# A hybrid attention and recurrence layer: the K/V block leaves PSUM bank by bank, and the second half of the recurrence gets its gates later

## The chip, the cores and the metric

The kernel runs on one core of one Trainium2 chip. The metric is the device time of one execution in microseconds (us), lower is better. The core has five engines with an instruction queue each: TensorE (PE in the profile; its weight loads are listed as PEld), VectorE (DVE), ScalarE (ACT), GpSimd (POOL) and SyncE (SP), which here only issues the DMA transfers of weights, x and the output. SBUF is the working memory. PSUM, where TensorE writes its products, has eight banks of 512 float32 values a partition.

## The reference

One layer of an encoder on 512 tokens of width 2048: a norm, one wide input projection, attention and a gated linear recurrence side by side, and one output projection.

```python
h = rms_norm(x, norm_w)
proj = jnp.einsum('bsd,de->bse', h, w_in)
q, k, v, g_attn, xr, g_lru = jnp.split(proj, SPLITS, axis=-1)
attn_out = attention_group(q, k, v, q_norm_w, k_norm_w)
lru_out = lru_group(xr, conv_w, conv_b, lru_wa, lru_ba, lru_wx, lru_bx, lru_lambda)
mixed = jnp.concatenate([rms_norm(attn_out, attn_norm_w) * jax.nn.silu(g_attn),
                         rms_norm(lru_out, lru_norm_w) * jax.nn.silu(g_lru)], axis=-1)
return x + jnp.einsum('bse,ed->bsd', mixed, w_out)
```

Attention has 8 query heads and 2 key/value heads of 128 features; q and k are normed head by head and rotated. The recurrence has 1024 features in 8 blocks of 128: a convolution over four tokens gives xc, then for each of two directions

```python
r = jax.nn.sigmoid(block_diag(xf, wa) + ba)
i = jax.nn.sigmoid(block_diag(xf, wx) + bx)
log_a = -LRU_C * r * jax.nn.softplus(-lam)
a = jnp.exp(log_a)
mult = jnp.sqrt(-jnp.expm1(2.0 * log_a))
return linear_scan(a, mult * (i * xf), reverse)
```

and the two directions are added. All of it is float32.

## The kernel before, in words

**Products.** Each float32 operand is split into a high and a low part, and `mm3` (L111 to L114) adds up three products, high by high, high by low and low by high. Weights come in as chunks of 256 rows by 512 columns (`wraw`, L155); ScalarE writes each half's high part (`wh`, L168) and VectorE subtracts it to get the low part (`wl`, L169). `wh` and `wl` have four slots, so two chunks are in hand at a time: a chunk can be split once the chunk two before it has been multiplied.

**Projections.** `proj_tok` (L271, by `tok_block`, L259) makes a block of 512 output columns for all tokens: four PSUM banks, the tag `pj`, one bank for each tile of 128 tokens. It runs over eight chunks, and in each chunk over the four token tiles; it yields after each tile, which is one *step* of six products. So a projection has 32 steps, and its four banks are finished in the last four steps, one after the other. There are only four `pj` banks: the next projection's first step needs the first bank empty, its second step the second bank, and so on. The block from column `C_K` holds the keys (256 columns) and the values (256 columns).

**The order.** TensorE runs its instructions as they are written (`manual_schedule`, L602). `weave(fill, chain)` (L274) interleaves: the chain yields how many steps of the projection go before its next piece. On ScalarE, VectorE and GpSimd a planner orders the instructions when the program is built: among those that it takes to be ready, the one with the best rank goes next. The rank is the place in the program, unless `tc.high_priority` gives a better one: without a number the very best, with `AHEAD` 600 instructions earlier. The queues then run in that order, each in turn; an instruction that is not ready holds those behind it.

**Around the change.** While the K/V block is projected (`a3`), the second half of the recurrence runs woven in (`lru_half(1, a2)`, L650): blocks 4 and 5 as one pair, 6 and 7 as the next (`lru_pair`, L338). A pair first gets its convolution (ScalarE L349, VectorE L354) and its operands split (`gh`, `gl` L344 and L345; `ch`, `cl` L359 and L360). Then each of its two blocks yields its number of steps and has twelve products for the gates into the `mm` banks, which ScalarE empties by four sigmoids (L371); VectorE multiplies `i` by xc (L375). Then ScalarE does four tanh (L380), four exponentials (L386) and two square roots (L390), each kind with a table load, and VectorE the rest of the pair: L393, L394, four scans (L397) and two additions (L401). ScalarE squares the result (L405) and GpSimd adds it up (L406). The steps are

```python
yield from lru_pair(4 * half + b, xrs[bs], grs[bs], (6 + 2 * half, 4, 8, 4)[bs])
```

so in the second half 8, 4, 8 and 4 steps go before the gates of its four blocks, and eight steps come behind the last gates.

**The K/V block leaves PSUM.** `kv(a3)` (L478) starts when the projection is done. It has the best rank, and takes two operations on ScalarE and one on VectorE from each bank: the keys scaled by the token's 1/rms (L432, 256 columns), the high part of the values (L485, 256 columns) and their low part (L486, VectorE, from the same bank). Then `norm_rope` (L438) norms and rotates the keys: squares on ScalarE (L446), 1/rms on GpSimd (L220, L221) and the rotation on VectorE (L451, L453, L459, L460). It is ranked behind the scans of the recurrence, which stand earlier in the program. `kv` is woven into the next projection, Q (`a4`): twenty steps, then the keys of head 0 are transposed on TensorE (L471, one product for each token tile), two more steps, then those of head 1.

Of the kernel before, what the change touches and what calls it, by code (L numbers as in the profile page):

```python
# [13 lines left out]
ALU = mybir.AluOpType  # L14
# [37 lines left out]
def hybrid_kernel(  # L52
# [62 lines left out]

# [1 line left out]
    ident = const([P, P], "ident")  # L117
# [25 lines left out]
    def columns(dst, src):  # L143
        """Vectors staged a row each, turned into a column each."""
        n = src.shape[0]
        pt = mm()
        nc.tensor.transpose(pt[:, :n], src, ident[:n, :n])
        with tc.high_priority():
            nc.vector.tensor_copy(dst, pt[:, :n])
# [3 lines left out]

# [1 line left out]
    def wraw(w, r0, c0, nk=1):  # L155
        """w[r0 : r0 + 2 * P, c0 : c0 + 512], in nk transfers."""
        raw = sb.tile([P, 2, SEQ], F32, tag="wr", bufs=3, name=nm("wr"))
        src = w[r0 : r0 + 2 * P, c0 : c0 + SEQ].rearrange("(k p) e -> p k e", p=P)
        for k in range(nk):
            ks = slice(k * 2 // nk, (k + 1) * 2 // nk)  # L160
            nc.sync.dma_start(raw[:, ks, :], src[:, ks, :])
            yield raw

    def wsplit(raw, k):
        """A row block's float32r high and low parts."""
        hi = sb.tile([P, SEQ], F32R, tag="wh", bufs=4, name=nm("wh"))
        lo = sb.tile([P, SEQ], F32R, tag="wl", bufs=4, name=nm("wl"))
        nc.scalar.copy(hi, raw[:, k, :])  # L168
        nc.vector.tensor_sub(lo, raw[:, k, :], f(hi))  # L169
        return hi, lo  # L170
# [5 lines left out]

# [1 line left out]
    xh, xl = [None] * KT, [None] * KT  # L178
    ssq = const([P, NT, KT // 2], "ssq")

    def xload(c, nk=1):
        """Two column blocks of x, in nk transfers."""
        xc = b4(shape=(P, NT, 2 * P))
# [34 lines left out]
    def rsqrt_mean(dst, src, n, width):  # L218
        """dst = (src / n + EPS) ** -0.5, for few elements."""
        nc.gpsimd.tensor_scalar(dst, src, 1.0 / n, EPS, op0=ALU.mult, op1=ALU.add)  # L220
        nc.gpsimd.tensor_tensor(dst, dst, nhalf[:, :width], op=ALU.pow)  # L221
# [14 lines left out]

# [1 line left out]
    # Generators that yield after every six products, to have other work woven in.  # L238
    def proj_feat(c0, acc, first=None):
        """Four [feature, token] blocks from column c0 on."""  # L240
        acc += [pj() for _ in range(4)]
# [17 lines left out]
    def tok_block(acc, w, r0, c0, lh, ll, nk):  # L259
        """Four [token, feature] blocks of 512 columns of w from c0 on."""  # L260
        acc += [pj() for _ in range(NT)]
# [12 lines left out]
    def weave(fill, chain):  # L274
        """chain yields how many steps of fill go before its next piece."""
        for n in chain:
# [6 lines left out]

# [1 line left out]
    c1 = const([P, 2 * NB], "c1")  # L285
    c2 = const([P, 2 * NB], "c2")

    def lru_consts():
        # c1 = -8 softplus(-lambda), c2 = c1 / 2, by log1p(y) = 2 atanh(y / (2 + y))
        lam = vec[:, R_LAM : R_LAM + 2 * NB]  # L290
# [13 lines left out]
        nc.vector.tensor_mul(acc, acc, s)  # L304
        # softplus(-lam) = 2 acc + max(-lam, 0)
        nc.vector.tensor_scalar(a, lam, -1.0, 0.0, op0=ALU.mult, op1=ALU.max)
# [7 lines left out]
    def evac_bc(acc):  # L314
        """Feature-major blocks out of PSUM, scaled by each token's 1 / rms."""
        res = []
# [7 lines left out]
    def lru_half(half, acc):  # L324
        """Four blocks of the recurrence, two at a time."""
        grs = []
# [7 lines left out]
        for b in range(0, 4, 2):  # L334
            bs = slice(b, b + 2)
            yield from lru_pair(4 * half + b, xrs[bs], grs[bs], (6 + 2 * half, 4, 8, 4)[bs])

    def lru_pair(n0, xrs, grs, steps):  # L338
        """Blocks n0 and n0 + 1; yields before each block's gate products."""
        xcs, cs, rs, is_, ths = [], [], [], [], []  # L340
# [21 lines left out]
        for b, n in enumerate((n0, n0 + 1)):  # L362
# [11 lines left out]
            i = is_[b]  # L374
            nc.vector.tensor_mul(i, i, xcs[b][:, None, :].broadcast_to([P, 2, SEQ]))  # L375
        for b, n in enumerate((n0, n0 + 1)):
            ths.append(b4())
# [5 lines left out]
        for b, n in enumerate((n0, n0 + 1)):  # L383
            for d in range(2):
                j, r = d * NB + n, rs[b][:, d, :]
                last = nc.scalar.activation(r, r, AF.Exp, scale=c1[:, j : j + 1])  # L386
        # sqrt(1 - a^2) = (1 + a) sqrt(-tanh(log_a / 2))
        with tc.issue_after(last.ins):
# [18 lines left out]

# [1 line left out]
    rq = const([P, NT, 2, HD], "rq")  # L409
# [15 lines left out]

    def evac_tok(acc, cols):
        """Token-major blocks out of PSUM, scaled by each token's 1 / rms."""
        res = []
        with tc.high_priority():
            for t in range(NT):  # L430
                e = ev()
                nc.scalar.activation(  # L432
                    e[:, :cols], acc[t][:, :cols], AF.Identity, scale=rstd[:, t : t + 1]
                )
                res.append(e)
        return res

    def norm_rope(es, nh, tab):  # L438
        """The heads of every token tile normed and rotated, in place."""
        es = [e[:, : nh * HD].rearrange("p (h d) -> p h d", d=HD) for e in es]  # L440
# [26 lines left out]
    def turn(rot, h):  # L467
        """The four token tiles of head h, transposed and split."""
        pt = mm()
# [7 lines left out]

    def kv(acc):  # L478
        es = evac_tok(acc, NKV * HD)
        with tc.high_priority():  # L480
            for t in range(NT):
                vv = acc[t][:, NKV * HD :]
                vt = const([P, 2, NKV * HD], f"v{t}", F32R)
                vh[t], vl[t] = vt[:, 0, :], vt[:, 1, :]
                nc.scalar.activation(vh[t], vv, AF.Identity, scale=rstd[:, t : t + 1])  # L485
                nc.vector.scalar_tensor_tensor(  # L486
                    vl[t], vv, rstd[:, t : t + 1], f(vh[t]), op0=ALU.mult, op1=ALU.subtract
                )
        rot = norm_rope(es, NKV, rk)
        for h in range(NKV):  # L490
            yield (20, 2)[h]
# [7 lines left out]
    def turned(rot, h):  # L499
        """Head h's queries, transposed and split."""  # L500
        q = b4(F32R)
# [3 lines left out]
    def weights(q, g, t):  # L505
        """Softmax over the keys for token tile t."""
        qh, ql = q
# [21 lines left out]
    def values(h, half, pth, ptl):  # L529
        """Head h's sums over the keys, for half of the tokens."""  # L530
        gs = slice(h // G * HD, (h // G + 1) * HD)
# [15 lines left out]
    def attention(rots):  # L547
        """All heads, as a pipeline over their token tiles."""
        qs, ps_, pts = {h: turned(rots[0], h) for h in range(2)}, {}, {}
# [18 lines left out]

# [1 line left out]
    mh, ml = [None] * 16, [None] * 16  # L570

    def gate(gs, dst, row):
        """dst *= w * silu(g), in place, in steps."""
        ss = []
# [13 lines left out]
    def group_rstd(sums, name, n):  # L588
        """Per-token 1 / rms of a head group from its feature-major sums of squares."""
        pr = mm()  # L590
# [8 lines left out]

# [1 line left out]
    # TensorE runs its instructions in the order in which they stand here.  # L601
    ctx.enter_context(tc.manual_schedule(engines={mybir.EngineType.PE}))  # L602
# [45 lines left out]
    rope_consts()  # L648
    fill = proj_tok(C_K, a3)
    weave(fill, lru_half(1, a2))  # L650
    drain(fill)
    fill = proj_tok(C_Q, a4)
    weave(fill, kv(a3))
    drain(fill)

    rots = [norm_rope(evac_tok(a4, SEQ), G, rq)]
    drain(proj_tok(C_Q + SEQ, a5))
    rots.append(norm_rope(evac_tok(a5, SEQ), G, rq))

# [44 lines left out]
def _rope_table():  # L704
    """[SEQ, 2, HD]: the cosines, and the sines with the sign that goes with the swapped halves."""
    s = np.arange(SEQ)
# [36 lines left out]
```

## Time and profile before

| | |
|---|---|
| three runs | 683.22, 682.63, 683.08 us |
| median | 683.08 us |
| profiled execution, span from first to last instruction | 681.7 us |
| profiled execution, whole time | not listed beside the span; the median is 1.4 us above the span |
| TensorE products | busy 671.0 us (98%) |
| VectorE / ScalarE / GpSimd | busy 409.0 / 318.8 / 79.7 us |
| granted TensorE clock, mean | 0.996 of full speed |

The profile is one execution taken by the hardware profiler. Its page gives the busy time of each engine, the span in 40 slices, the DMA queues, the chain of work that ended last, and the costliest groups of instructions. Beside the page, the trace answers questions: who waited for whom (engine and line waited for: us in total, times, longest), a timeline of one engine (start in us, duration in us, engine, line, operation, result <- operands, shapes, count, and in brackets how long the engine had been idle and what ended that), and the busy time of each engine in a stretch of time. L12 is line 12 of the kernel. Names are the pools' tags: `pj` and `mm` are PSUM banks, `ev`, `b` and `k` are buffers in SBUF, `v` the split values. A product's duration overlaps the next one's, so the pace of TensorE is read from the starts.

### The profile page before, as it was taken

To read this page: it belongs to the slowest core of one execution; us is meant where nothing else is said; L and a number is where in the kernel's file an instruction comes from. 1 tells how busy PE (TensorE), PEld (TensorE's weight loads), DVE (VectorE), ACT (ScalarE), POOL (GpSimd) and SP (SyncE) were. 2 spreads that over 40 slices of the span, in tenths; PEclk is the share of its full clock that TensorE was granted. 3 is DMA by queue.
4 is the path that set the end of the run, shared out by engine and by line. 5 is a ranking of instruction groups with operands and counts; after the bars stand their busy time and mean duration, and the time that the engine had idled before them with its cause. 6 is when DMAs were issued, how large, how long until landed. Compare 5 with 4: busy or idle time off the path is not lost.

```text
span 681.7 us, 8574 instructions
## 1 busy us (share of the span) xinstructions
PE 671.0 (98%) x3149; PEld 557.3 (82%) x3149; DVE 409.0 (60%) x713; ACT 318.8 (47%) x593; POOL 79.7 (12%) x84
## 2 busy tenths in 40 slices
PE   8999999999899999999999999999999999999997
PEld 6888888787688888888888888888888888888885
DVE  5869697979693824846744674577475334443342
ACT  4433898698934427434634543464452222222220
POOL 0000001111260302211211111112000000000000
PEclk9999999999899999999999999999999999999999
DMA  8842252221213222321212121212256362522411
GB/s 281 278 131 86 72 154 69 87 62 63 92 63 124 93 94 92 93 63 62 62 63 93 38 86 62 62 62 68 86 171 203 109 229 92 154 94 92 158 59 63
DMA packets 43626, 71.01 MB, mean 104 GB/s; under 512 B 2760, under 2 KB 12864, under 8 KB 43584
## 3 DMA queue, kind: packets, MB, share of 16 engines
q1 hardware_dynamic: 43552, 70.45, 32.2%
q8 instruction: 25, 0.41, 0.3%
q14 instruction: 17, 0.14, 0.1%
q10 hardware_dynamic: 32, 0.01, 0.0%
HBM read 66.25 MB, written 4.19 MB: 103 GB/s over the span
## 4 chain that ended last, share of the span: by engine, by line
PE 90%; DVE 5%; ACT 2%; issue 1%; DMA 1%; SPq 0%; DVEq 0%; ACTq 0%
PE pj L112 26%; PE pj L113 26%; PE pj L114 26%; PE mm L114 3%; PE mm L113 3%; PE mm L112 3%; PE mm L524 2%; DVE k L354 1%; DVE b L397 1%; DVE wl L169 1%; PE mm L194 1%; DVE b L394 1%; DMA b<-in_x_dram 1%; PE mm L471 1%; DVE hs L401 0%
## 5 line engine op out<-in xcount | busy, mean ns | idle before, releaser
L169 DVE TENSOR_TENSOR wl<-wr,wh 128x512 fp32r<-128x512 f32 x208 | 144.4, 706 | 157.3 <-ACT wh L168 157.0
L168 ACT CAST wh<-wr 128x512 fp32r<-128x512 f32 x208 | 127.2, 620 | 208.6 <-PE pj L114 154.7
L112 PE MATMUL pj<-wh,x 128*128 128x512 f32 x448 | 175.3, 391 | 2.6 <-DVE v L486 2.6
L113 PE MATMUL pj<-wl,x 128*128 128x512 f32 x448 | 175.0, 391 | 0.0
L114 PE MATMUL pj<-wh,x 128*128 128x512 f32 x448 | 174.9, 390 | 0.0
L112 PE MATMUL pj<-x,wh 128*128 128x512 f32 x384 | 153.3, 399 | 0.0
L114 PE MATMUL pj<-x,wl 128*128 128x512 f32 x384 | 150.3, 391 | 0.0
L113 PE MATMUL pj<-x,wh 128*128 128x512 f32 x384 | 150.2, 391 | 0.0
L112 PEld LDWEIGHTS pj<-wh,x 128*128 128x128 f32 x448 | 84.5, 189 | 20.7 <-DVE v L486 3.1
L114 PEld LDWEIGHTS pj<-wh,x 128*128 128x128 f32 x448 | 84.5, 189 | 17.7
L113 PEld LDWEIGHTS pj<-wl,x 128*128 128x128 f32 x448 | 84.4, 188 | 17.4
L114 PEld LDWEIGHTS pj<-x,wl 128*128 128x128 f32 x384 | 72.4, 188 | 15.7
L112 PEld LDWEIGHTS pj<-x,wh 128*128 128x128 f32 x384 | 72.4, 189 | 14.1 <-issue 0.2
L113 PEld LDWEIGHTS pj<-x,wh 128*128 128x128 f32 x384 | 72.5, 189 | 13.9 <-issue 0.2
L526 ACT CAST b<-mm 128x512 fp32r<-128x512 f32 x32 | 18.8, 587 | 71.8 <-PE mm L524 71.8
L517 POOL TENSOR_SCALAR k<-k,sm 128x512 f32<-128x512 f32 x32 | 26.2, 818 | 157.4 <-DVE sm L516 139.1
L512 DVE TENSOR_REDUCE mx<-mm 128x1 f32<-128x512 f32 x32 | 22.0, 687 | 30.3 <-PE mm L114 30.2
L406 POOL TENSOR_TENSOR hsum<-hsum,b 128x512 f32<-128x512 f32 x7 | 18.7, 2675 | 117.7 <-ACT b L405 117.7
L527 DVE TENSOR_TENSOR b<-mm,b 128x512 fp32r<-128x512 f32 x32 | 22.0, 687 | 10.5 <-ACT b L526 10.5
L515 ACT ACTIVATE k<-mm,mx 128x512 f32<-128x512 f32 x32 | 22.1, 692 | 4.2 <-DVE mx L512 3.9
L354 DVE SCALAR_TENSOR_TENSOR k<-ev,vec,k 128x511 f32<-128x511 f32 (+1 forms) x24 | 20.0, 832 | 2.2 <-ACT k L349 2.0
L371 ACT ACTIVATE b<-mm,vec 128x512 f32<-128x512 f32 x32 | 20.5, 688 | 0.9 <-PE mm L114 0.9
(136 smaller groups left out, 695.6 us busy)
## 6 DMA issues: line engine op xcount, KB each, us to landing
wr<-in_w_in_dram SPq DMA_DIRECT2D x71, 512.0 KB, 3.4
wr<-in_w_out_dram SPq DMA_DIRECT2D x32, 512.0 KB, 3.6
k<-in_x_dram SPq DMA_DIRECT2D x16, 256.0 KB, 5.2
out_dram<-k SPq DMA_DIRECT2D x16, 256.0 KB, 3.5
b<-in_x_dram SPq DMA_DIRECT2D x7, 512.0 KB, 8.1
k<-in_lru_wa_dram SPq DMA_DIRECT2D x8, 128.0 KB, 3.4
k<-in_lru_wx_dram SPq DMA_DIRECT2D x8, 128.0 KB, 2.8
b<-in_x_dram SPq DMA_DIRECT2D x2, 256.0 KB, 4.6
```

What stands on the lines that cost most here:

```text
L112: nc.tensor.matmul(acc, lh, rh, start=start, stop=False)
L113: nc.tensor.matmul(acc, lh, rl, start=False, stop=False)
L114: nc.tensor.matmul(acc, ll, rh, start=False, stop=stop)
L168: nc.scalar.copy(hi, raw[:, k, :])
L169: nc.vector.tensor_sub(lo, raw[:, k, :], f(hi))
L354: nc.vector.scalar_tensor_tensor(xc[:, d0:d1], xr[:, d0 + o : d1 + o], v1(R_CW + j * NB + n), xc[:, d0:d1], op0=ALU.mult, op1=ALU.add,)
L371: nc.scalar.activation(dst[:, d, :], pg, AF.Sigmoid, bias=v1(bias + d * NB + n))
L512: nc.vector.tensor_reduce(mx, sc, axis=AX.X, op=ALU.max, negate=True)
L515: nc.scalar.activation(p, sc, AF.Exp, bias=mx, accum_out=sm)
L517: nc.gpsimd.tensor_scalar(p, p, sm, 0.0, op0=ALU.mult, op1=ALU.add)
L526: nc.scalar.copy(pth[:, :, tt], p3)
L527: nc.vector.tensor_sub(ptl[:, :, tt], p3, f(pth[:, :, tt]))
```

## The change

Three things change.

1. `evac_tok` takes a whole bank of 512 columns in one ScalarE operation, for K/V as for Q. The values are split later, out of SBUF: a ScalarE copy and a VectorE subtraction for each token tile, which stand behind `norm_rope` in the program.
2. The four K/V operations belong to the end of the K/V projection (`kv_proj`), and the last pair of the recurrence yields 99 steps after its gates: the rest of the projection and the four operations stand ahead of its tanh, exponentials, square roots and scans in the program.
3. The steps before the gates of the second half are 10, 4, 8 and 4. Six steps are left behind the last gates.

```diff
+            steps = ((6, 4, 8, 4), (10, 4, 8, 4))[half][bs]
+            yield from lru_pair(4 * half + b, xrs[bs], grs[bs], steps, 99 if half and b else 0)
...
             i = is_[b]
             nc.vector.tensor_mul(i, i, xcs[b][:, None, :].broadcast_to([P, 2, SEQ]))
+        yield rest
         for b, n in enumerate((n0, n0 + 1)):
             ths.append(b4())
...
-                nc.scalar.activation(
-                    e[:, :cols], acc[t][:, :cols], AF.Identity, scale=rstd[:, t : t + 1]
-                )
+                nc.scalar.activation(e, acc[t], AF.Identity, scale=rstd[:, t : t + 1])
...
-    def kv(acc):
-        es = evac_tok(acc, NKV * HD)
-        with tc.high_priority():
-            for t in range(NT):
-                vv = acc[t][:, NKV * HD :]
-                vt = const([P, 2, NKV * HD], f"v{t}", F32R)
-                vh[t], vl[t] = vt[:, 0, :], vt[:, 1, :]
-                nc.scalar.activation(vh[t], vv, AF.Identity, scale=rstd[:, t : t + 1])
-                nc.vector.scalar_tensor_tensor(
-                    vl[t], vv, rstd[:, t : t + 1], f(vh[t]), op0=ALU.mult, op1=ALU.subtract
-                )
+    def kv(es):
         rot = norm_rope(es, NKV, rk)
+        for t in range(NT):
+            vv = es[t][:, NKV * HD :]
+            vt = const([P, 2, NKV * HD], f"v{t}", F32R)
+            vh[t], vl[t] = vt[:, 0, :], vt[:, 1, :]
+            nc.scalar.copy(vh[t], vv)
+            nc.vector.tensor_sub(vl[t], vv, f(vh[t]))
...
+    def kv_proj():
+        yield from proj_tok(C_K, a3)
+        kvs.extend(evac_tok(a3))
+
+    weave(kv_proj(), lru_half(1, a2))
+    fill = proj_tok(C_Q, a4)
+    weave(fill, kv(kvs))
     drain(fill)
```

The calls of `evac_tok` for Q lose their column count and stay what they were.

More of the change, by code (lines that the diff above doesn't have):

```diff
@@ L335, in lru_half, with lru_pair @@
             bs = slice(b, b + 2)
-            yield from lru_pair(4 * half + b, xrs[bs], grs[bs], (6 + 2 * half, 4, 8, 4)[bs])
-    def lru_pair(n0, xrs, grs, steps):
+            steps = ((6, 4, 8, 4), (10, 4, 8, 4))[half][bs]
+            yield from lru_pair(4 * half + b, xrs[bs], grs[bs], steps, 99 if half and b else 0)
+    def lru_pair(n0, xrs, grs, steps, rest):
         xcs, cs, rs, is_, ths = [], [], [], [], []
@@ L424, in rope_consts, with evac_tok @@
                 nc.vector.tensor_mul(dst[:, t], dst[:, t], wb)
-    def evac_tok(acc, cols):
+    def evac_tok(acc):
         res = []
@@ L648, in hybrid_kernel @@
     rope_consts()
-    fill = proj_tok(C_K, a3)
-    weave(fill, lru_half(1, a2))
+    kvs = []
+    def kv_proj():
[4 more added lines that the diff above has]
+    weave(fill, kv(kvs))
     drain(fill)
[L652 to L656, printed above, removed]
+    rots = [norm_rope(evac_tok(a4), G, rq)]
     drain(proj_tok(C_Q + SEQ, a5))
-    rots.append(norm_rope(evac_tok(a5, SEQ), G, rq))
+    rots.append(norm_rope(evac_tok(a5), G, rq))
     def all_gates():
```

## The prediction

> **What bounds the kernel now.** I read the page first, for the engine that is full and for the chain that ended last.
>
> ```profile
> span 681.7 us, 8574 instructions
> PE 671.0 (98%) x3149; PEld 557.3 (82%) x3149; DVE 409.0 (60%) x713; ACT 318.8 (47%) x593; POOL 79.7 (12%) x84
> PE 90%; DVE 5%; ACT 2%; issue 1%; DMA 1%; SPq 0%; DVEq 0%; ACTq 0%
> ```
>
> TensorE is the bound, and no product is removed. What a change can win is TensorE's waiting. So next the waits of TensorE alone:
>
> ```profile
> PE pj L112 <- DVE v L486: 2.6, 1, 2.6
> PE mm L113 <- DVE k L360: 1.6, 1, 1.6
> ```
>
> Both lie in the K/V projection or at its end. The timeline of TensorE tells what they and a shorter one cost, from start to start.
>
> ```profile
> 133.33 0.40 PE L112 MATMUL mm<-k,k 128*128 128x512 f32 x1
> 135.32 0.51 PE L113 MATMUL mm<-k,k 128*128 128x512 f32 x1 [1.59 <-DVE k L360]
> ...
> 156.75 0.39 PE L114 MATMUL pj<-wh,x 128*128 128x512 f32 x1
> 157.59 0.50 PE L112 MATMUL mm<-k,k 128*128 128x512 f32 x1 [0.45 <-ACT b L371]
> ...
> 160.44 0.39 PE L112 MATMUL pj<-wh,x 128*128 128x512 f32 x1
> ...
> 171.09 0.39 PE L114 MATMUL pj<-wh,x 128*128 128x512 f32 x1
> 174.12 0.63 PE L112 MATMUL pj<-wh,x 128*128 128x512 f32 x1 [2.64 <-DVE v L486]
> ...
> 177.88 0.39 PE L112 MATMUL pj<-wh,x 128*128 128x512 f32 x1
> ...
> 203.06 0.60 PE L471 MATMUL mm<-ident,ev 128*128 128x128 f32 x4
> ```
>
> Pace: the 48 products of the last eight K/V steps start from 160.44 to 171.09, so 10.65 / 47 = 0.227 us each, and a step is 1.36 us. Lost: 135.32 - 133.33 - 0.227 = 1.76; 157.59 - 156.75 - 0.227 = 0.61; at the hand-over to Q 174.12 - 171.09 - 0.227 = 2.80; and then nine products take 177.88 - 174.12 = 3.76 us where nine at the pace take 2.04, so 1.72 more, because the granted clock fell after the long wait and only there. Sum 6.89 us, 1.0% of the span: the most that the change can win here.
>
> Whether that reaches the end is decided at 203.06, the first transposes of the keys, twenty Q steps on. They need the rotated keys, which come from this chain on ScalarE and VectorE:
>
> ```profile
> 166.85 0.72 ACT L380 ACTIVATE b<-b,c 128x512 f32<-128x512 f32 x1 [0.94 <-DVE b L397]
> 168.51 0.63 ACT L405 ACTIVATE b<-hs 128x512 f32<-128x512 f32 x1 [0.93 <-DVE hs L401]
> 169.05 0.71 ACT L380 ACTIVATE b<-b,c 128x512 f32<-128x512 f32 x1
> 169.78 1.28 ACT L386 ACT_TABLE_LOAD   x1
> 171.07 0.72 ACT L386 ACTIVATE b<-b,c 128x512 f32<-128x512 f32 x1
> 171.70 1.12 ACT L168 CAST wh<-wr 128x512 fp32r<-128x512 f32 x2
> 172.73 0.47 ACT L432 ACTIVATE ev<-pj,rstd 128x256 f32<-128x256 f32 x1
> 173.10 0.46 ACT L485 ACTIVATE v<-pj,rstd 128x256 fp32r<-128x256 f32 x1
> ```
>
> ```profile
> 148.32 1.29 DVE L169 TENSOR_TENSOR wl<-wr,wh 128x512 fp32r<-128x512 f32 x2 [0.22 <-ACT wh L168]
> ...
> 173.59 0.48 DVE L486 SCALAR_TENSOR_TENSOR v<-pj,rstd,v 128x256 fp32r<-128x256 f32 x1
> ...
> 181.00 2.36 DVE L393 SCALAR_TENSOR_TENSOR b<-b,b 128x1024 f32<-128x1024 f32 x2 [2.29 <-ACT b L390]
> ...
> 200.97 1.40 DVE L459 TENSOR_TENSOR ev<-ev,rk 128x256 f32<-128x256 f32 x1
> 202.40 0.42 DVE L460 TENSOR_TENSOR ev<-ev,sq 128x256 f32<-128x256 f32 x1
> ```
>
> The last rotation ends at 202.40 + 0.42 = 202.82, the transposes begin at 203.06: the keys are ready with 0.24 us to spare. Two windows (columns: stretch, length, then busy us of PE, PEld, DVE, ACT, POOL, the clock, DMA) show how full the chain is:
>
> ```profile
> 164.70:181.00 16.30, 13.66 (x53) 10.79 (x53) 9.48 (x12) 14.38 (x25) 2.45 (x2) 0.90 0.23 74
> 181.00:202.80 21.80, 21.80 (x98) 18.06 (x97) 21.73 (x37) 10.04 (x28) 14.74 (x10) 1.00 0.26 84
> ```
>
> From the last sigmoid to the first square root ScalarE is busy 14.38 of 16.30 us; then VectorE works 21.73 of 21.80 us on scans, weight splits and the rotation. **So two chains end together at 203 us**, and the wait at 174.12 has been hiding that the second one is as long as the first.
>
> **The change part by part.**
>
> *Gates two steps later.* Twelve more products stand ahead of each gate group of the second half: 12 x 0.227 = 2.72 us. The second group then starts at 133.33 + 2.72 = 136.05, behind the L360 that let TensorE go on at 135.32; the 1.76 us go. What is late next there: L360 could slip 0.7 us before the wait returns. The fourth group starts at 156.75 + 0.23 - 1.76 + 2.72 = 157.94, after its PSUM bank came free at 157.59; the 0.61 go. But two steps taken from behind the last gates means that weights are wanted sooner. The sixth chunk is first used in step 21, which moves from behind the third gates to ahead of them: wanted at 136.05 + 2.72 + 6 x 1.36 = 146.9, its first half is split at 148.32 + 0.65 = 149.0 before. A new wait between 0 (its slots are free 1.9 us sooner, so the planner may put it forward) and 2.1 us; between the two I take 1.0. The K/V block ends at 171.09 + 0.23 - 1.76 - 0.61 + 1.0 = 169.95.
>
> *One operation a bank.* These groups carry the price:
>
> ```profile
> L432 ACT ACTIVATE ev<-pj,rstd 128x512 f32<-128x512 f32 x8 | 5.4, 678 | 1.5 <-PE pj L114 1.5
> L486 DVE SCALAR_TENSOR_TENSOR v<-pj,rstd,v 128x256 fp32r<-128x256 f32 x4 | 1.9, 484 | 1.8 <-ACT v L485 1.7
> L451 DVE TENSOR_TENSOR ev<-ev,rr 128x256 f32<-128x256 f32 x4 | 1.6, 405 | 0.0
> ```
>
> Gone are four L432 of 476 ns, four L485 and four L486; the first bank is free after one operation, 0.68 us instead of 172.73 to 174.07, which is 1.34 us. Added later are four ScalarE copies and four VectorE subtractions of 256 columns, about 0.41 us each by the L451 row (estimate: same size, SBUF operands). Nothing on TensorE waits for them until the attention; their cover is idle ScalarE time (10.04 busy of 21.80). VectorE has no such cover: ahead of the last rotation they cost 4 x 0.41 = 1.6 us of the second chain, behind it nothing. They rank behind the rotation, but may be ready first.
>
> *K/V ahead of the exponentials.* The order on the queue was already by best rank, among what is ready; before, L380, the table load and one L386 went first because the bank was not yet ready in the planner's eyes. With two steps fewer behind the last gates, the bank comes 2.72 us earlier beside them, about as long as L386's load and first exponential with half of L168 x2 (1.28 + 0.72 + 0.6). I take the first bank right behind the last tanh, 169.76, free at 170.4: TensorE waits 0.5 us. I take one exponential with its load (2.0 us) before the second bank, free at 170.4 + 2.0 + 0.7 = 173.1 where TensorE wants it at 171.8: 1.3 us. Each is under the 1.76 us after which the clock held, so no slow products. Bounds: 0, and the 2.80 + 1.72 of before.
>
> So Q starts, waits counted in, at 169.95 + 0.5 + 1.3 = 171.7, against 177.88 - 2.04 = 175.84 before. TensorE reaches the keys' transposes 4.1 us sooner, at 198.9. DMAs: no transfer is added; SP's weight loads follow L169 and come sooner with it.
>
> *The second chain.* The square root that starts it ends at 181.00. Saved ahead of it: the pairs of K/V operations start 0.72 us apart with the exponentials left out (172.73, 173.10 and 0.36 more), a single one takes 0.68 and less where it overlaps the next, so 0.2 to 0.5 us in all; and the two idle waits of 0.94 and 0.93 us can be filled with weight splits or banks, 0 to 1.9 us. Against it, Q's third chunk may be split ahead of the root, 1.1 us. Between -2.4 and +0.9 I take -1.6, nearer the filled waits, since weight splits are free to fill them. The 21.8 us behind it have no gap, so the last rotation moves as a whole: 202.82 - 1.6 = 201.2. Into it may come one more weight chunk (1.29, because Q is ahead) and the four subtractions (1.6): 0 to 2.9, of which I take 0.6, as both rank or come late: 201.8.
>
> **Sum.** TensorE stands ready at 198.9 and can start the fourth transpose, that of the last token tile, only at 201.85; before, it began some 0.3 us behind the first (four take 0.60 in the row at 203.06), at 203.36: -1.5 us. But TensorE has waited 201.85 - 198.9 - 0.3 (three tiles done early) = 2.7 us, as long as the 2.80 that cost the clock. I charge the same 1.72. The net is +0.2 us on a span of 681.7. The page gives no time of that execution beside its span; the median lies 1.4 above it, and I add the difference to the median: **683.3 us**. Behind the transposes TensorE waits nowhere in the list, so what is gained or lost there stays to the end.
>
> **The rivals.** A change under 0.2% (1.37 us) is about what a measurement of this kernel can't tell from none; I count it as the same.
>
> *A: the keys' wait stays short of the clock.* All as above without the 1.72: -1.5 us, 681.6. For it: 1.76 us did no harm in the row at 135.32. Against it: 2.80 did. The Trainium skill ("TensorE: Matmul & The Clock Gate", Part 1) says that the clock is halved after an idle window of about 3.4 us that runs free of the kernel, so a wait of under 3 us may or may not hit; the trace agrees as far as its slow products fill about 3.4 us (174.12 to 177.54).
>
> *B: the keys come in time.* TensorE keeps its 4.1 us: 679.0, and up to the 6.89 without the waits I took (676.2). It needs the last L460 to end by about 199.2, 3.6 us earlier. For it: 200.97 shows an L459 of 1.40 us where 128x256 takes 0.41, while GpSimd was busy, so 1.0 us may vanish. Against it: scans rank ahead of the rotation, and the window has 0.07 us of idle time.
>
> *C: the rotation ends later, on the slower side.* One mechanism: the values' subtractions and a weight chunk get ahead of the rotation on VectorE and the root moves little. With the 2.9 whole and the root at -1.6 it ends at 204.1: 204.1 + 0.05 - 203.36 + 1.72 = +2.5 us, 685.6; with the root at +0.9 as well, 688.1. It decides once the last L460 ends after 203.0.
>
> *D: the exponentials stay in front.* The planner goes by readiness and lets load and L386 pass as before. First bank at 172.73, free at 173.41, TensorE waits 173.41 - 169.95 = 3.5 us with the slow clock, Q starts at 175.1 instead of 175.84: -0.7 us, 682.4, with the keys at about 202.4 no earlier.
>
> **How the numbers follow.** Forecast 0.36, A 0.16, B 0.20, C 0.19, D 0.09. Faster: B, half of A, and 0.04 from the edges of the forecast and D, 0.32. Slower: C less 0.02, and 0.09 of the forecast where the root gains less: 0.26. The same: the rest, 0.42. Range 678.8 to 686.2: it takes in B's centre and C's centre, and leaves out B beyond 4.3 us (0.08) and C beyond 3.1 us (0.07). The forecast's own range is 682.5 to 685.8, by the root's bounds of -2.4 and +0.9.
>
> **What would show it.** Right: no wait for L360 near 135; no L486-like wait at the hand-over, and the Q projection's first products at full clock; a wait of TensorE at L471 for L460 of 2 to 4 us, slow products behind it, and VectorE without a gap from about 179 to 202. Wrong: no wait at L471 (B), a wait there but a full clock (A), the values' subtractions ahead of L460 and its end after 203.0 (C), table load and L386 in front of the first bank (D). A wait over 3 us for the sixth chunk's L169 near 147 would mean that the two steps cost a slow clock of their own, which no term here holds.

## The result, and the profile after

The changed kernel takes 687.05 us (median of four runs, 686.53 to 688.27) against 683.15 of the kernel before (four runs, 682.63 to 684.33). The ratio is 1.0057, 95% interval 1.0042 to 1.0073: slower by about 0.6%, and by 0.4% at least. The profiled execution spans 684.7 us against 681.7. This time the whole time of that execution is known, 686.53, so 1.8 us lie outside the span.

From the page of the changed kernel: the engines, and the chain that ended last.

```profile
PE 672.6 (98%) x3149; PEld 557.0 (81%) x3149; DVE 408.9 (60%) x713; ACT 318.4 (46%) x593; POOL 76.6 (11%) x84
PE 85%; DVE 8%; ACT 4%; issue 1%; DMA 1%; SPq 0%; ACTq 0%; DVEq 0%
```

The busy times are those of before, but for 1.6 us of TensorE and 3.1 us of GpSimd. In the chain, TensorE has gone from 90 to 85% and VectorE from 5 to 8%: the chain now runs over VectorE and ScalarE as far as the keys' transposes near 205 us, where before TensorE took it over at the hand-over to Q, at 174 us. The waits of TensorE from 110 to 210 us (us in total, times, longest):

```profile
PE mm L471 <- DVE ev L460: 3.5, 2, 2.1
PE mm L112 <- ACT b L372: 1.7, 3, 0.9
PE pj L113 <- DVE wl L169: 0.8, 2, 0.5
PE pj L112 <- ACT ev L434: 0.5, 1, 0.5
```

The wait for the subtraction L360 and the long one at the hand-over to Q (L486) are gone, and in their place stands one for the rotated keys at L471. The timeline of TensorE prices each, from start to start, against the pace of 0.227 us (numbers of lines have moved by one or two: the copy `ch` and the subtraction `cl`, L359 and L360 before, are L360 and L361, sigmoids L372, tanh L382, exponentials L388, square roots L392, first step of the scan stage L395):

```profile
136.82 0.39 PE L114 MATMUL mm<-k,k 128*128 128x512 f32 x1
138.07 0.50 PE L112 MATMUL mm<-k,k 128*128 128x512 f32 x1 [0.86 <-ACT b L372]
...
158.42 0.39 PE L114 MATMUL pj<-wh,x 128*128 128x512 f32 x1
159.04 0.50 PE L112 MATMUL mm<-k,k 128*128 128x512 f32 x1 [0.24 <-ACT b L372]
...
159.61 0.40 PE L114 MATMUL mm<-k,k 128*128 128x512 f32 x1
160.66 0.50 PE L112 MATMUL mm<-k,k 128*128 128x512 f32 x1 [0.65 <-ACT b L372]
...
170.80 0.39 PE L114 MATMUL pj<-wh,x 128*128 128x512 f32 x1
171.67 0.49 PE L112 MATMUL pj<-wh,x 128*128 128x512 f32 x1 [0.49 <-ACT ev L434]
172.63 0.50 PE L113 MATMUL pj<-wl,x 128*128 128x512 f32 x1 [0.47 <-DVE wl L169]
...
200.73 0.39 PE L471 MATMUL mm<-ident,ev 128*128 128x128 f32 x2
203.20 0.33 PE L471 MATMUL mm<-ident,ev 128*128 128x128 f32 x1 [2.08 <-DVE ev L460]
204.95 0.47 PE L471 MATMUL mm<-ident,ev 128*128 128x128 f32 x1 [1.42 <-DVE ev L460]
205.08 0.77 PE L112 MATMUL pj<-wh,x 128*128 128x512 f32 x1
...
208.15 0.39 PE L113 MATMUL pj<-wl,x 128*128 128x512 f32 x1
```

The sum of it. The two profiled executions did not start alike: the VectorE row at 126.14 (126.53 before), shown further down and ahead of all that differs, comes 0.39 us earlier after the change. The last line of the table counts from that row.

| | before | after |
|---|---|---|
| in the K/V block | 1.76 + 0.61 = 2.37 | 1.02 + 0.39 + 0.82 = 2.23 |
| hand-over to Q | 2.80 + 1.72 slow = 4.52 | 0.64 + 0.73 = 1.37 |
| the rest of the way to the keys' transposes | 0.17 | 1.52, of it 0.51 for a weight split at 196.06 |
| lost at the transposes | 0 | 3.99 of waiting and 1.40 of slow products = 5.39 |
| TensorE reaches the transposes, in all | 203.06 | 200.73 |
| the same, counted from that row | 76.53 | 74.59, so 1.94 sooner |

(3.99 is 205.08 - 200.73 less the 0.36 that the four transposes take before, 203.06 to 203.42; 1.40 is seven products in 3.07 us for 1.59 at the pace, less 0.08 that the kernel before has there too.) So 1.94 won and 5.39 lost: 3.45 us. From that row to the end the profiled executions differ by 3.4 us; of that the spans show 3.0, because of the 0.39 us ahead of it.

Why are the keys late? On ScalarE and VectorE of the changed kernel:

```profile
141.74 0.62 ACT L360 CAST k<-k 128x512 fp32r<-128x512 f32 x1 [1.99 <-DVE k L355]
142.26 0.68 ACT L372 ACTIVATE b<-mm,vec 128x512 f32<-128x512 f32 x1
...
143.35 0.69 ACT L372 ACTIVATE b<-mm,vec 128x512 f32<-128x512 f32 x1
...
145.15 0.73 ACT L382 ACTIVATE b<-b,c 128x512 f32<-128x512 f32 x1
...
165.89 0.63 ACT L407 ACTIVATE b<-hs 128x512 f32<-128x512 f32 x1 [0.93 <-DVE hs L403]
166.43 0.67 ACT L372 ACTIVATE b<-mm,vec 128x512 f32<-128x512 f32 x1
```

```profile
126.14 1.21 DVE L395 SCALAR_TENSOR_TENSOR b<-b,b 128x1024 f32<-128x1024 f32 x1
...
156.07 2.36 DVE L395 SCALAR_TENSOR_TENSOR b<-b,b 128x1024 f32<-128x1024 f32 x2 [3.36 <-ACT b L392]
...
181.27 1.23 DVE L395 SCALAR_TENSOR_TENSOR b<-b,b 128x1024 f32<-128x1024 f32 x1 [3.43 <-ACT b L392]
...
193.63 2.38 DVE L169 TENSOR_TENSOR wl<-wr,wh 128x512 fp32r<-128x512 f32 x2
...
200.86 1.28 DVE L169 TENSOR_TENSOR wl<-wr,wh 128x512 fp32r<-128x512 f32 x2
...
203.48 0.41 DVE L485 TENSOR_TENSOR v<-ev,v 128x256 fp32r<-128x256 f32 x1
...
204.15 0.41 DVE L485 TENSOR_TENSOR v<-ev,v 128x256 fp32r<-128x256 f32 x1
204.48 0.41 DVE L460 TENSOR_TENSOR ev<-ev,sq 128x256 f32<-128x256 f32 x1
```

and the same places in the kernel before, first on ScalarE, then on VectorE:

```profile
139.81 0.69 ACT L371 ACTIVATE b<-mm,vec 128x512 f32<-128x512 f32 x1
142.05 0.62 ACT L359 CAST k<-k 128x512 fp32r<-128x512 f32 x1 [1.55 <-DVE k L354]
...
163.48 0.63 ACT L405 ACTIVATE b<-hs 128x512 f32<-128x512 f32 x1 [1.44 <-DVE hs L401]
164.02 0.67 ACT L371 ACTIVATE b<-mm,vec 128x512 f32<-128x512 f32 x1
```

```profile
126.53 1.22 DVE L393 SCALAR_TENSOR_TENSOR b<-b,b 128x1024 f32<-128x1024 f32 x1
...
153.58 1.23 DVE L393 SCALAR_TENSOR_TENSOR b<-b,b 128x1024 f32<-128x1024 f32 x1 [3.36 <-ACT b L390]
```

The row at 126.14 (126.53 before) is the same piece of work of the first half, ahead of all that differs; I count from it, and so does the table below. I call it the common event. From there the scan stage of blocks 4 and 5 starts after 29.93 us (27.05 before), the last sigmoid after 40.29 (37.49), the last scan stage after 55.13 (54.47), and the last rotation ends after 78.75 (76.29). In the changed kernel L360, a copy for the *last* pair, stands in ScalarE's queue ahead of two sigmoids of the *first* pair and waits 1.99 us for VectorE there. In the kernel before, the same copy waits 1.55 us (142.05), but behind the first pair's last sigmoid (139.81). In both kernels the very last sigmoid starts right behind the square of block 4's result (165.89 and 163.48), which waits for the addition that ends that block's scans; so a late first pair makes the last sigmoid late. (Of the three kinds that follow the sigmoids, only exponentials and square roots have a table load in the traces, at 148.26 and 153.69 after; the tanh follow the sigmoids without one.) The last rotation is 2.46 us later: 0.66 from the last scan stage's start, and 1.80 from that start to the rotation's end (204.89 - 181.27 = 23.62 against 21.82), into which a fourth weight chunk (1.28) and two subtractions of the values (0.67) have come.

### The profile page after: what moved, and what is told of

The parts are those of the page before. It is cut to its first block, busy times and chain, and to the rows that moved or that the text cites. A ratio compares the mean times of both kernels' runs of the same rounds, so it can differ in the third digit from the quotient of the medians.

```text
span 684.7 us, 8563 instructions
## 1 busy us (share of the span) xinstructions
PE 672.6 (98%) x3149; PEld 557.0 (81%) x3149; DVE 408.9 (60%) x713; ACT 318.4 (46%) x593; POOL 76.6 (11%) x84
## 4 chain that ended last, share of the span: by engine, by line
PE 85%; DVE 8%; ACT 4%; issue 1%; DMA 1%; SPq 0%; ACTq 0%; DVEq 0%
PE pj L112 24%; PE pj L114 24%; PE pj L113 24%; PE mm L114 3%; PE mm L113 3%; PE mm L112 3%; PE mm L520 2%; DVE b L399 2%; DVE wl L169 2%; PE mm L194 1%; DVE k L355 1%; DVE b L396 1%; DVE b L395 1%; PE mm L471 1%; ACT b L388 1%
## 5 line engine op out<-in xcount | busy, mean ns | idle before, releaser
L169 DVE TENSOR_TENSOR wl<-wr,wh 128x512 fp32r<-128x512 f32 x208 | 147.4, 721 | 161.1 <-ACT wh L168 160.2
L408 POOL TENSOR_TENSOR hsum<-hsum,b 128x512 f32<-128x512 f32 x7 | 13.5, 1931 | 118.9 <-ACT b L407 118.9
L372 ACT ACTIVATE b<-mm,vec 128x512 f32<-128x512 f32 x32 | 20.9, 688 | 2.3 <-DVE b L399 1.4
L320 DVE TENSOR_TENSOR ev<-pj,rbc 128x512 f32<-128x512 f32 x24 | 16.4, 688 | 6.5 <-PE pj L114 6.3
```

The source lines that it names most:

```text
L320: nc.vector.tensor_mul(e, a, rbc)
L372: nc.scalar.activation(dst[:, d, :], pg, AF.Sigmoid, bias=v1(bias + d * NB + n))
```

## The experiments

All kernels compute the whole layer. Ratios are against the kernel before, each with a 95% interval.

### Which part does it

*The gates alone*: the kernel before with the new steps.

```diff
-            (6 + 2 * half, 4, 8, 4)[bs]
+            ((6, 4, 8, 4), (10, 4, 8, 4))[half][bs]
```

> The kernel before with one part of the change: 10, 4, 8 and 4 steps in the second half. Theory 'gates': the later gates put the second group's sigmoids behind a ScalarE copy that waits for VectorE, the scans of blocks 4 and 5 start some 2.5 us later (156.07 in the profile after, 153.58 before), and with them everything to the rotated keys; then this part alone costs about 2.5 us, 685.6, with a wait at the keys' transposes. Theory 'VectorE work': the loss comes from what stands ahead of the last rotation (two of the values' subtractions, a weight chunk), so this part alone is within 0.7 us of before, 683.

686.15 us, ratio 1.0042 (1.0027 to 1.0056). Its waits of TensorE:

```profile
PE mm L471 <- DVE ev L460: 2.7, 2, 1.9
PE pj L112 <- DVE v L486: 2.4, 1, 2.4
...
```

*The bank alone*: the changed kernel with the old steps.

```diff
-            steps = ((6, 4, 8, 4), (10, 4, 8, 4))[half][bs]
+            steps = ((6, 4, 8, 4), (8, 4, 8, 4))[half][bs]
```

> The changed kernel with the old steps 8, 4, 8 and 4: whole-bank operations and the new place in the program stay. Theory 'gates': the scans of blocks 4 and 5 start near 153.6 again, the bank hand-over is 0.5 to 0.7 us shorter than before, the keys are ready near 202.8; 682.3, between 681.0 and 684.0. Theory 'VectorE work': the two subtractions and a chunk still stand ahead of the rotation, the transposes wait some 2 us with slow products behind, 685.5 or more.

683.49 us, ratio 1.0005 (0.9996 to 1.0014). Its waits:

```profile
PE pj L112 <- ACT ev L434: 2.0, 1, 2.0
PE pj L113 <- DVE wl L169: 1.8, 1, 1.8
...
```

Of the two theories the one named "gates" holds: the steps alone make the slower kernel and its wait at L471. The bank alone makes no difference: the hand-over costs 2.15 us instead of 4.52, and Q then runs into a wait for a weight split that VectorE has not come to (195.17 to 197.50, 2.1 us more than the pace), with slow products behind it. Nor does the K/V block's new place in the program bring the banks forward by itself: in this run the exponentials' table load (169.22) and the first exponential still stand ahead of the first bank (172.17), as before, while with the gates alone, at the old place, the first bank (170.19) stands ahead of the load (172.36).

### Is the wait at the keys the whole loss

*The keys' transposes after 26 steps of Q* instead of 20, in the changed kernel, and as a control in the kernel before:

```diff
-            yield (20, 2)[h]
+            yield (26, 2)[h]
```

> The changed kernel, but the keys' transposes come after 26 steps of Q instead of 20, which is 8.2 us more cover and moves no work off an engine. If the 2.24 and 1.64 us of waiting at L471 and the 1.5 us of slow products behind are the loss, all 5.4 us go: 681.7, between 681.0 and 682.5, faster than before. If the late chain only comes out elsewhere (the Q block's banks, the attention's first scores), it stays above 685.

> The kernel before, with the keys' transposes after 26 steps of Q instead of 20. It is the control for the run that moved them in the changed kernel. If that run's gain is the wait of TensorE at L471 alone, this one stays at the kernel before, 683.1 (ratio 1.000 within 0.002), since the kernel before had 0.24 us to spare there. If the place is better by itself, it comes near 681.5 (ratio 0.998).

The changed kernel comes to 681.20 us, ratio 0.9977 (0.9968 to 0.9986); the kernel before to 682.83, ratio 0.9996 (0.9986 to 1.0006). The waits of the first of them:

```profile
PE mm L112 <- ACT b L372: 1.8, 3, 0.9
PE pj L113 <- DVE wl L169: 1.3, 3, 0.5
...
```

The span is 679.2 instead of 684.7. Of these 5.5 us 0.9 lie ahead of the common event (125.25 and 126.14); behind it 4.6 are won, which are the 5.39 lost at the transposes less 0.62 for a new wait for a weight split (199.85 to 200.70), to within 0.2. The place is no better by itself, as the control shows. So the change's own gain was there all along, and one consumer that came too early took more than all of it.

### What stands ahead of the rotation

*The values' subtractions behind the last rotation*, in the changed kernel:

```diff
-            nc.vector.tensor_add(e, e, sq)
+            added[0] = nc.vector.tensor_add(e, e, sq)
...
+            with tc.issue_after(added[0].ins):
-            nc.vector.tensor_sub(vl[t], vv, f(vh[t]))
+                nc.vector.tensor_sub(vl[t], vv, f(vh[t]))
```

> The changed kernel with the values' four subtractions queued behind the last rotation on VectorE. Theory 'VectorE work': two subtractions of 0.34 us pace leave the way, the last rotation ends 0.7 us sooner, 686.3; if the planner puts more than the subtractions in order, down to 685. Theory 'gates': no more than these 0.7 us, 686.3 to 687. More than 2 us would mean that the subtractions were the cause.

686.01 us, ratio 1.0045 (1.0032 to 1.0058), which can't be told from the changed kernel's 1.0057. The last rotation ends 78.33 us after the common event instead of 78.75, and the wait at the transposes is 3.57 instead of 3.99 us. Worth 0.4 us; not the cause.

### Which pair

The second half's steps once more, one pair at a time. First the second pair later, the first where it was:

```diff
-            steps = ((6, 4, 8, 4), (10, 4, 8, 4))[half][bs]
+            steps = ((6, 4, 8, 4), (8, 4, 10, 4))[half][bs]
```

> The changed kernel with steps of 8, 4, 10 and 4: the first pair's gates stand where they stood before, the second pair's two steps later as in the change. Theory 'late sigmoids' (the first pair's gates come behind L360 on ScalarE, and its four scans and all behind them start 2.5 us late): the scans of blocks 4 and 5 start within 0.7 us of the kernel before's, the last scan stage near 180, the last rotation ends by 203.0, TensorE waits at most 1 us at L471, 681.5 to 683.5 us. Theory 'too few steps behind the last gates' (six in place of eight press exponentials, banks and scans together): it is as slow as the changed kernel, 686 to 687, with the last rotation near 204.9.

Then the first pair later, the second where it was:

```diff
-            steps = ((6, 4, 8, 4), (10, 4, 8, 4))[half][bs]
+            steps = ((6, 4, 8, 4), (10, 4, 6, 4))[half][bs]
```

> The changed kernel with steps of 10, 4, 6 and 4: the first pair's gates two steps later, the second pair's where they stood, eight steps behind the last gates. Theory 'late sigmoids': the first pair's scans start 2 us later than before, TensorE waits 2 us or more at L471, 685.5 to 687. Theory 'too few steps behind the last gates': the harm goes, 682.5 to 683.5, with no wait at L471.

And the second pair later with the keys' transposes after 26 steps:

```diff
-            steps = ((6, 4, 8, 4), (10, 4, 8, 4))[half][bs]
+            steps = ((6, 4, 8, 4), (8, 4, 10, 4))[half][bs]
...
-            yield (20, 2)[h]
+            yield (26, 2)[h]
```

> The changed kernel with steps of 8, 4, 10 and 4, and the keys' transposes after 26 steps. No wait at L471 under either theory, since six steps are 8.2 us. 'Late sigmoids': K/V gives up what it waits at L360 but keeps the hand-over, and 680.0 to 681.5 us come out, under the 681.2 of the run that only moved the keys or level with it. 'Too few steps': 681 to 682, with the wait for the weight split L169 of about 1 us still there.

Counted from the common event, in us:

| kernel | first pair's scan stage | last scan stage | last rotation ends | TensorE at the keys | time | ratio |
|---|---|---|---|---|---|---|
| before | 27.05 | 54.47 | 76.29 | 76.53 | 683.15 | 1 |
| after | 29.93 | 55.13 | 78.75 | 74.59 | 687.05 | 1.0057 (1.0042 to 1.0073) |
| gates alone | 29.93 | 57.23 | 79.79 | 76.45 | 686.15 | 1.0042 (1.0027 to 1.0056) |
| second pair later | 27.06 | 56.29 | 79.91 | 76.38 | 687.22 | 1.0060 (1.0044 to 1.0076) |
| first pair later | 29.93 | 55.55 | 79.12 | 77.74 | 684.69 | 1.0028 (1.0016 to 1.0039) |
| second pair later, 26 steps | 27.07 | 56.29 | 79.92 | | 684.02 | 1.0011 (1.0001 to 1.0021) |

I expected the second pair to be harmless; it is as bad as the whole change. The other two forecasts missed as well: the first pair later came out between the ranges of its two theories (685.5 to 687 and 682.5 to 683.5), and the second pair later with 26 steps above both of its own (680.0 to 681.5 and 681 to 682). Either pair alone makes the last rotation late, by 3.62 and 2.83 us, and the two don't add up (2.46 together). Why they don't is not shown. A reading of the trace, which no run tests: with the second pair later, the square of block 5's result, too, stands ahead of the last sigmoid on ScalarE and waits 2.66 us there for the first pair's addition, so this kernel as well loses by what stands in front.

```profile
167.30 0.63 ACT L407 ACTIVATE b<-hs 128x512 f32<-128x512 f32 x1 [2.66 <-DVE hs L403]
167.84 0.67 ACT L372 ACTIVATE b<-mm,vec 128x512 f32<-128x512 f32 x1
```

In the same kernel TensorE also waits at the hand-over, since the last tanh still stand in front of the first bank:

```profile
PE pj L112 <- ACT ev L434: 3.9, 2, 2.9
PE mm L471 <- DVE ev L460: 2.9, 2, 1.5
...
```

That wait stays with 26 steps (2.9 us), so they win back 3.2 us by the medians and bring this kernel only about level with the kernel before. With the first pair later, the rotation is late, but TensorE comes late too, after a wait of 3.0 us for a gate bank, so that only 0.9 us shows at L471:

```profile
PE mm L112 <- ACT b L372: 4.5, 3, 3.0
...
PE mm L471 <- DVE ev L460: 0.9, 1, 0.9
```

What these kernels have in common is the end: where TensorE waits at L471, the span is the end of the last rotation plus 478.3 to 478.4 us and the slow products behind (684.7 - 204.89 - 1.40 = 478.4 after; 683.5 - 205.17 = 478.3 for the gates alone; 684.0 - 205.62 = 478.4 for the first pair; 685.2 - 205.21 - 1.69 = 478.3 for the second).

### Why the first pair is late

The last pair's convolution and splits (L345 to L361) rank 300 instructions ahead of their place. Lowered to 15:

```diff
-            with tc.high_priority(AHEAD // 2):
+            with tc.high_priority(AHEAD // (40 if n0 == 6 else 2)):
```

> The changed kernel with one rank lowered: the convolution and the splits of the last pair (L345 to L361 for blocks 6 and 7) rank 15 instructions ahead of their place instead of 300. Steps stay 10, 4, 8 and 4. That takes L360 of the last pair, which waits for VectorE, from in front of the first pair's last sigmoids. Theory 'queueing' (the first pair is late because its sigmoids stand behind that L360): the first tanh comes by 143.5 and the scan stage of blocks 4 and 5 by 154.5, where the changed kernel has 145.15 and 156.07; the last rotation ends by 203.5, TensorE waits under 2 us at L471, 683 to 685.5 us. Theory 'dose' (the first pair is late because its gates themselves come 2.7 us later): the scan stage stays after 155.5, the rotation after 204.5, and 686 to 687.5 us. A price that either may pay: the last pair's operands come later, and TensorE can wait for L361 ahead of the third gates.

> The same lowered rank, with the keys' transposes after 26 steps. No wait at L471 in any case. 'Queueing': the waits for L372 (1.8 us in the run with 26 steps alone) shrink as well, and it comes to 679.5 to 681.0, under the 681.2 of that run. 'Dose': 681 to 682, no better than that run, with the waits for L372 still there.

At a rank of 15: 687.86 us, ratio 1.0071 (1.0055 to 1.0087), and with 26 steps 685.20, ratio 1.0036 (1.0022 to 1.0049): both far from what I expected in time. But in the first of them the scan stage of blocks 4 and 5 starts 26.06 us after the common event, a microsecond sooner than before the change, though the gates come two steps later. So the first pair is late by the queue, not by its gates. The price went elsewhere: the last pair's L360 now stands behind the first pair's square roots, TensorE waits for it, and the wait at L471 is still there.

```profile
PE mm L112 <- ACT k L360: 4.2, 1, 4.2
PE mm L113 <- DVE k L361: 2.2, 2, 1.9
PE mm L471 <- DVE ev L460: 2.1, 2, 1.4
```

A rank of 30 puts that L360 between: behind all sigmoids of the first pair, ahead of its exponentials.

```diff
-            with tc.high_priority(AHEAD // 2):
+            with tc.high_priority(30 if n0 == 6 else AHEAD // 2):
```

> The changed kernel with the convolution and splits of the last pair ranked 30 instructions ahead of their place (300 in the changed kernel, 15 in the run before): all sigmoids of the first pair now stand in front of the last pair's L360, and that L360 still stands in front of the first pair's exponentials, so that TensorE need not wait for the last pair's operands. Theory 'first pair': the last rotation is late because the first pair is. Then the scan stage of blocks 4 and 5 starts by 154.8 (156.07 in the changed kernel), the last rotation ends by 203.7 instead of 204.89, the wait at L471 falls under 2 us, 683.5 to 685.5. Theory 'second pair': the last gates come two steps later in any case, and they alone make the last rotation late; the scan stage of blocks 4 and 5 comes sooner and the last rotation stays after 204.5, 686 to 687.5.

> The same rank with the keys' transposes after 26 steps. No wait at L471. 'First pair': waits for L372 fall from 1.8 us to 1 or less, 680.0 to 681.0. 'Second pair': the waits stay as in the run with 26 steps alone, 681.0 to 682.0. If the last pair's operands come late, a wait of 1 us or more for L360 or L361 near 148 shows, and 682 or more.

With 20 steps: 685.67 us, ratio 1.0042 (1.0029 to 1.0054). With 26 steps: 679.94 us, ratio 0.9959 (0.9946 to 0.9973), faster than both kernels and close to what theory 'first pair' expected (680.0 to 681.0); the waits for L372 fell to 0.9 us with it. Against the 0.9977 of 26 steps alone the two intervals still touch. ScalarE in the first of them, where L360 now waits 0.31 us and no sigmoid stands behind it:

```profile
141.53 0.69 ACT L372 ACTIVATE b<-mm,vec 128x512 f32<-128x512 f32 x1
142.53 0.62 ACT L360 CAST k<-k 128x512 fp32r<-128x512 f32 x1 [0.31 <-DVE k L355]
```

Its scan stage of blocks 4 and 5 starts after 28.78 us (29.93 in the changed kernel), the last one after 53.97 (0.50 sooner than in the kernel before), the last rotation ends after 77.60. That is 1.15 us won on the rotation. But TensorE won as much, 73.43 instead of 74.59, and the lost time at the transposes stays at 3.95 us. It lies between the two theories: the first one's bounds for the scan stage, the rotation and the time are missed by 0.3, 0.2 and 0.2 us, the second one's for rotation and time by 0.6 and 0.3, and the wait under 2 us that the first expected didn't come. With the queue mended the rotation is 1.31 us later than in the kernel before, only by the work ahead of it: the last scan stage starts sooner, and 23.6 us follow instead of 21.8. So the change loses even with the last scan stage in time; it needs the keys' transposes moved.

One step later instead of two, with 26 steps:

```diff
-            steps = ((6, 4, 8, 4), (10, 4, 8, 4))[half][bs]
+            steps = ((6, 4, 8, 4), (9, 4, 8, 4))[half][bs]
-            yield (20, 2)[h]
+            yield (26, 2)[h]
```

> The changed kernel with steps of 9, 4, 8 and 4 (one step later instead of two) and the keys' transposes after 26 steps. 'Dose' is about proportional: the wait for L361 near 134 falls from 1.76 to 0.4, the waits for L372 from 1.8 to about 1, the first pair comes 1.4 us late instead of 2.7; 680 to 681.5 us. 'Queueing' goes by which instruction stands in front: with the sigmoids behind L360 as with ten steps, it is no better than 681.2; with the load of the exponentials' table in front of the first bank, a wait of 2 us or more for L434 returns at the hand-over and it is 682 to 683.5.

682.62 us, ratio 0.9996 (0.9987 to 1.0005). The wait for L361 falls to 0.2 us, and the last of the expected cases happened: the exponentials' table load and first exponential stand ahead of the first bank, and TensorE waits 2.4 us for L434 at the hand-over. What comes out goes by the order in the queues, not in proportion to the steps.

## Why the prediction was wrong, point by point

Rival C's outcome happened: the keys come later, TensorE waits for them, and products behind the wait are slow. The step that failed is the second chain: the prediction had the square root that starts the last scan stage 1.6 us earlier, and it came 0.66 us later. Where I compare times below, both count from the common event, since the profiled execution after was 0.39 us ahead there. Step by step:

- **"The 1.76 us go", "the 0.61 go": failed.** The subtraction holds nobody up near 135 any more, but 2.23 us come back as waits for the sigmoids that empty the gate banks. The sixth chunk's wait, for which 1.0 was put in, does not exist. K/V's last product starts 44.66 us after the common event, 44.56 before: the block won nothing, where the sum had it end 1.4 us sooner.
- **K/V ahead of the exponentials: held.** Banks at 170.95 and 172.13, table load behind them; waits of 0.64 and 0.73 us where 0.5 and 1.3 were forecast (the second for a weight split, not for a bank), and no slow products. The reason was the steps, as the prediction took it, since with the new place in the program alone the exponentials stay in front.
- **TensorE at the transposes: 4.1 us sooner forecast, 1.94 measured.** 2.2 us less, most of it from the first step and from 0.51 us of waiting for a weight split near 196.
- **The second chain, "-1.6" for the square root: the step that decides.** The last scan stage started 0.66 us later than before, 2.3 us off the forecast. I summed only what the change saves behind the last sigmoid. That saving is real: from the last sigmoid to the last scan stage 14.84 us instead of 16.98. But the last sigmoid itself comes 2.80 us later, because the first pair fell behind; I had followed the gates on TensorE and not their sigmoids in ScalarE's queue, where L360 of the next pair stands ahead. With that order mended (rank 30) the last scan stage came 0.50 us sooner than before. So of the 2.3 us that order is worth 1.2, and 1.1 are a saving that I took too large; the bounds of -2.4 and +0.9 hold both values.
- **"+0.6" for chunk and subtractions ahead of the last rotation: 1.80 measured**, one chunk and two of the four subtractions. 2.3 + 1.2 are the 3.5 us by which the last rotation missed its forecast: 1.0 us sooner than before was forecast, 2.46 later was measured.
- **The clock at L471, 1.72: 1.40 measured.** So the forecast's own sum, +0.2, becomes 0.2 + 3.5 - 0.3 = +3.4, which is what the executions differ by from the common event on. That TensorE would wait at the transposes, and pay for it with slow products, was right; the rotation's time was not.
- **The addition to the median, 1.4**, should have been 1.8: the profiled execution of before was then 0.4 us above the median, and that of after 0.5 below its own. With the 3.0 of the spans, these make the 3.9 us between the medians.
- **The chances.** C had 0.19, between the prices of 685.6 and 688.1 that it gave; the result lies there. The bound from which it decides, the last L460 ending after 203.0, was passed by 1.9 us as the profile has it (204.89), and by 2.3 counted from the common event. That the time falls between its prices is in part luck: of its mechanism, subtractions and a chunk ahead of the rotation, the runs show 1.80 of the 2.9 us, and the late first pair, which moved the root, is in none of the rivals. The range ended at 686.2, inside C.

## What to carry to other kernels

Where two chains end together, work out for both when they arrive, and give the consumer room first: six steps more before the keys' transposes turned a change of +0.57% into one of -0.23%, and nothing else in the change had to be touched. When products are moved, follow what empties them through its own engine's queue: an instruction with a better rank that the planner takes to be ready can stand in front of it and wait (here 2 us for a copy whose gates TensorE reached some eight us later). What such an exchange does can't be read off its size: with 26 steps, rank 300, 30 and 15 gave -0.23%, -0.41% and +0.36%.

## What the runs showed of the hardware

The same wait of TensorE is followed by slow products in one execution and not in another. The kernel before waits 2.80 us at the hand-over and loses 1.72 after it. The same kernel with the keys six steps later has the same wait at the same place (172.45 - 169.44 - 0.227 = 2.78), and goes on at the pace:

```profile
172.45 0.50 PE L112 MATMUL pj<-wh,x 128*128 128x512 f32 x1 [2.62 <-DVE v L486]
172.78 0.40 PE L113 MATMUL pj<-wl,x 128*128 128x512 f32 x1
```

With the second pair later, a wait of 3.10 us cost nothing more, and with 26 steps beside it the same wait (3.05) was followed by slow products; in the bank-alone kernel, one of 2.10, ended at 197.50, was followed 1.3 us later by a slow spell, eight products of 0.42 us each (199.06 to 202.39). So the bound that the prediction drew between 1.76 and 2.80 us isn't one. In the kernel before, the changed one, the gates alone and the bank alone the slow spell lasted 3.0 to 3.6 us and cost 1.4 to 1.7. The Trainium skill ("TensorE: Matmul & The Clock Gate", Part 1) has the clock judged by windows of about 3.4 us that run free of the kernel, and lowered after an idle one. The length of these spells and their coming and going agree with that. (At rank 15 with 26 steps, behind waits of 4.38 and 2.45 us close together, products were slow for 5.2 us on end.) That the whole window is idle does not: 2.80 and 2.10 us of waiting were enough, and the measurement decides.

Apart from the clock, the core repeats itself closely from the common event on: in the changed kernel and in the two kernels made from it by moving the transposes or the subtractions, the last scan stage starts 55.13 us after the common event in all three. The event itself moves more, from 124.82 to 127.06 us over all these kernels, so spans of single executions are compared best from there.
